# Decayed running sum of a matmul: w loaded by slot over all quadrants, four heads in both first chunks, finer pieces of input

## The chip, the core and the metric

One core of a Trainium2 chip runs the whole kernel. Times are device microseconds (us) of one execution. "The span" is the time from the first to the last instruction in a profiled execution; it is some 2 us shorter than the run's time. In profile lines PE is TensorE and PEld its weight loads, DVE is VectorE, ACT ScalarE, POOL GpSimd and SP SyncE; `a<-b` reads "a is written from b", and [1.25 <-X] says that the engine idled for 1.25 us until X.

## The reference

```python
# x: (16, 2048, 1024), w: (1024, 1024), decay: (1024,), all float32
xw = x @ w
out[:, 0, :] = xw[:, 0, :]
for t in range(1, S):
    out[:, t, :] = decay[None, :] * out[:, t - 1, :] + xw[:, t, :]
```

A matmul is followed by a first-order recurrence along time, with one decay per column. The sixteen batches of 2048 times are cut into 64 chunks of 512 times. Two chunks make a group, and the 1024 output columns are cut into 8 heads of 128. A "step" is one head of one group: 8 slices of w by 2 chunks, 16 matmuls of 512 columns.

## The kernel before

w is cut into 16 slots: slot i is output half h = i // 8, parity e = i // 4 % 2 of its rows, and m = i % 4. x goes through GpSimd's DMA queue (stored as bf16), is turned by VectorE, and is parted into even and odd rows by a copy. w goes through SyncE's queue (the first two slots, kept in f32) and GpSimd's queue (the other fourteen, stored as bf16), into a staging room; a copy by VectorE or ScalarE then "settles" a slot into its place. In the kernel before, each load of w serves ONE quadrant of 32 partitions and several slots at once:

```python
def load_w(queue, h, e, m0=0, m1=M):                  # M = 4
    for q in range(NQ):                               # four transfers, 32 rows each
        pin(queue.dma_start(
            out=stage[h, e, m0][quad(q)].rearrange("p (m d) -> p m d", m=m1 - m0),
            in_=_ap(w, [[2 * D, P], [2 * P * D, m1 - m0], [1, CH]],
                    (q * CQ + m0 * 2 * P + e) * D + h * CH)))
...
for _ in range(34):                                   # warm-up of TensorE
    pin(nc.tensor.matmul(out=spare, lhsT=idle[:, 0:128], rhs=idle, start=True, stop=True))
load_w(nc.sync, 0, 0, 0, M // 2)
...
agenda = {                                            # order of the work off TensorE
    -99: "M0 M1 U0 U1 M2 M3 U2 U3 L L L W0 w1 E0 F0 G0 w3 W2 E1 F1 G1 W4 w5 W6 w7 E2 F2 D G2 E3 F3 G3 W8 W9 W10 W11",
    0: "w12 L L w13 P0 S0",
    ...
```

In the agenda M is a half chunk of x loaded, U a part of w loaded, L a later load of x, E or T a turn, F, G, X, Y a parting, W and w a settle by VectorE and by ScalarE, P, S, C and B the pairing, scan, completion and turning back of one tile. TensorE works on four heads of chunk 0, then on three of chunk 1, as the program gives one of its PSUM tiles of 128x512 to the squared decays; the fourth head's chunk 1 waits for a tile (1.25 us at 27.59 in before's trace).

## Time and profile before

| | before |
|---|---|
| median of 3 runs | 915.26 us (915.03 to 915.39) |
| span of the profiled run | 912.5 us |
| mean granted clock of TensorE | 0.996 |

The prediction shows the page's shares and TensorE's timeline. The DMA view of the first 40 us, in which each digit or number is one microsecond: the busy share of the 16 DMA engines in tenths, and GB/s.

```profile
DMA  0079899999999999999999999999999999999989
GB/s 0 16 241 153 145 226 119 173 180 193 197 197 200 203 181 190 150 191 190 190 195 183 202 201 211 179 187 196 195 196 197 197 195 196 197 196 127 162 97 122
```

From 5 us on the engines are busy for nine tenths or more (once eight), and from 9 to 35 us almost every microsecond moves 180 to 210 GB/s. GpSimd's first eight transfers, issued 0.56 to 0.72 us apart, land 0.66 to 0.93 us apart (6.12 to 11.20).

Then the page's DMA issues (name, queue, count, KB each as stored, and the median us from issue to landing), and two rows of GpSimd's timeline (start, length, line, what it issues, how many, and the wait ahead of it):

```profile
xb<-in_x_dram POOLq DMA_DIRECT2D x16, 128.0 KB, 5.0
ot<-in_w_dram POOLq DMA_DIRECT2D x12, 128.0 KB, 5.2
ot<-in_w_dram SPq DMA_DIRECT2D x4, 128.0 KB, 3.5
```

```profile
6.40 0.76 POOL L245 DMA_DIRECT2D ot<-in_w_dram  x1 [0.39 <-DMA xb<-in_x_dram]
12.01 4.69 POOL L105 DMA_DIRECT2D xb<-in_x_dram  x8
```

GpSimd issues its ninth transfer at 6.40, after the first has landed, and can begin chunk 1's x at 12.01. In the trace its transfers use eight semaphores in turn (99 to 106), and from the ninth on each issue waits for the semaphore of the one eight before it. So eight are in flight by the program's own waits, and the landing of the oldest sets when the next one starts.

And one row of the table by stage for the long middle (stretch, length, busy time and count of PE, PEld, DVE, ACT, POOL, then clock, DMA share and GB/s):

```profile
145.00:880.00 735.00, 731.42 (x3339) 333.20 (x3406) 676.99 (x480) 569.42 (x772) 537.42 (x599) 1.00 1.17 229
```

3406 weight loads in 735 us is a matmul every 0.2158 us, without a break.

### The profile page before, as it was taken

Reading aid. Unit: us, or ns where it says so; the run is one execution under the profiler, and the core shown is the slowest. Engines: PE = TensorE matmul, PEld = TensorE weight load, DVE = VectorE, ACT = ScalarE, POOL = GpSimd, SP = SyncE. Lnnn points to the kernel's source line nnn. Section 1 sums busy time; section 2 is a strip of 40 time slices with the busy share of each in tenths; the row PEclk is TensorE's granted clock in tenths of the full one; section 3 lists DMA queues with packets and bytes.
Section 4 is the critical chain, followed back from the end, with each engine's and each line's share of the span. In section 5 each row is a group of like instructions: output and inputs, shape, how many; then the busy total and the mean of one; then the engine's idle time right before and its main releaser. Section 6 shows DMA issues by size and latency. Waiting matters only on the chain.

```text
span 912.5 us, 11926 instructions
## 1 busy us (share of the span) xinstructions
PE 891.3 (98%) x4088; PEld 408.5 (45%) x4170; DVE 826.0 (91%) x613; ACT 685.8 (75%) x950; POOL 664.4 (73%) x764
## 2 busy tenths in 40 slices
PE   8899999999999999999999999999999999999995
PEld 4444444444444444444444444444444444444442
DVE  4999999999999999999999999999999999999986
ACT  3778887877877777778778778778778778777753
POOL 8688878777777777777677777777787776776552
PEclk9999999999999999999999999999999999999998
DMA  9999999999999999999999999999999999999668
GB/s 170 166 220 215 215 230 235 256 250 255 247 237 255 247 237 224 230 233 231 223 235 227 224 231 229 230 226 231 227 224 230 231 230 224 232 229 207 151 151 219
DMA packets 406253, 204.49 MB, mean 224 GB/s; under 512 B 12976, under 2 KB 405936, under 8 KB 406192
## 3 DMA queue, kind: packets, MB, share of 16 engines
q1 hardware_dynamic: 268848, 134.76, 59.5%
q0 software_dynamic: 137344, 68.96, 56.8%
q8 instruction: 32, 0.52, 0.2%
q14 instruction: 29, 0.24, 0.1%
HBM read 138.42 MB, written 134.22 MB: 299 GB/s over the span
## 4 chain that ended last, share of the span: by engine, by line
PE 90%; DMA 3%; POOL 2%; issue 2%; DVE 2%; ACT 1%; SPq 0%; DVEq 0%; POOLq 0%
PE ps L126 90%; DMA xb<-in_x_dram 2%; POOL xb L105 1%; DMA ot<-in_w_dram 1%; DVE so L194 1%; DVE xw L115 1%; POOL ot L245 1%; PE spare L126 0%; DMA out_dram<-ot 0%; DVE so L180 0%; POOL so L208 0%; ACT xt L123 0%; DVE ot L215 0%; POOL xs L174 0%; ACT xs L168 0%
## 5 line engine op out<-in xcount | busy, mean ns | idle before, releaser
L126 PE MATMUL ps<-xt,wsb 128*128 128x512 bf16 (+1 forms) x4011 | 874.2, 377 | 9.0 <-DVE so L194 2.6
L126 PEld LDWEIGHTS <-wsb 128*128 128x128 bf16 x4136 | 404.6, 98 | 485.7 <-issue 5.6
L174 POOL TENSOR_TENSOR xs<-h,xs 128x512 f32<-128x512 f32 (+1 forms) x193 | 245.3, 1271 | 195.5 <-ACT h L158 88.3
L168 ACT COPY xs<-ps 128x1024 f32<-128x1024 f32 (+1 forms) x193 | 191.6, 993 | 158.8 <-PE ps L126 149.3
L215 DVE STREAM_TRANSPOSE ot<-so 128x1024 f32<-128x1024 f32 (+1 forms) x264 | 302.7, 1184 | 1.9 <-POOL so L208 1.1
L208 POOL TENSOR_TENSOR so<-h,xs 128x512 f32<-128x512 f32 (+1 forms) x193 | 244.3, 1266 | 34.5 <-ACT h L158 18.1
L123 ACT COPY xt<-xw 128x2048 bf16<-128x2048 bf16 (+1 forms) x128 | 239.8, 1875 | 7.5 <-DVE xw L115 7.5
L105 POOL DMA_DIRECT2D xb<-in_x_dram x264 | 174.1, 660 | 2.0 <-POOLq L435 0.9
L158 ACT ACTIVATE h<-so,dec 128x512 f32<-128x512 f32 (+1 forms) x193 | 147.1, 763 | 36.0 <-DVE so L180 32.1
L115 DVE STREAM_TRANSPOSE xw<-xb 128x2048 f32<-128x2048 f32 (+1 forms) x66 | 146.7, 2222 | 6.1 <-DMA xb<-in_x_dram 6.1
L180 DVE TENSOR_TENSOR_SCAN so<-dec,keep,xs 128x512 f32<-128x512 f32 (+1 forms) x99 | 121.6, 1229 | 29.8 <-POOL xs L174 29.6
L180 DVE TENSOR_TENSOR_SCAN so<-dec,xs 128x512 f32<-128x512 f32 x94 | 114.8, 1222 | 31.3 <-POOL xs L174 28.2
L158 ACT ACTIVATE h<-ps,dec 128x512 f32<-128x512 f32 (+1 forms) x193 | 131.8, 683 | 0.0
L194 DVE TENSOR_TENSOR_SCAN so<-dec,ps 128x1024 f32<-128x1024 f32 x33 | 74.5, 2261 | 0.0
L194 DVE TENSOR_TENSOR_SCAN so<-dec,keep,ps 128x1024 f32<-128x1024 f32 (+1 forms) x33 | 73.4, 2225 | 0.0
L211 ACT COPY keep<-so 128x1 f32<-128x1 f32 x136 | 25.1, 187 | 0.3 <-DVE so L194 0.3
L173 ACT COPY so<-keep 128x1 f32<-128x1 f32 x99 | 19.0, 192 | 0.7 <-DVE ot L215 0.7
L171 POOL MEMSET so<- 128x1 f32 x94 | 11.0, 117 | 3.2 <-DVE ot L215 3.2
L262 PE MATMUL spare<-idle 128*128 128x512 bf16 x34 | 10.2, 473 | 1.2 <-DVE idle L259 1.2
L126 PE MATMUL spare<-xt,wsb 128*128 128x512 bf16 (+1 forms) x43 | 11.2, 359 | 0.1
L245 POOL DMA_DIRECT2D ot<-in_w_dram x16 | 9.0, 561 | 2.4 <-issue 0.7
L253 ACT COPY wsb<-ot 128x512 bf16<-128x512 bf16 x6 | 3.4, 615 | 5.7 <-DMA ot<-in_w_dram 5.7
(18 smaller groups left out, 20.3 us busy)
## 6 DMA issues: line engine op xcount, KB each, us to landing
out_dram<-ot SPq DMA_DIRECT2D x248, 512.0 KB, 10.6
xb<-in_x_dram POOLq DMA_DIRECT2D x248, 256.0 KB, 7.8
out_dram<-ot SPq DMA_DIRECT2D x12, 256.0 KB, 4.2
xb<-in_x_dram POOLq DMA_DIRECT2D x16, 128.0 KB, 5.0
ot<-in_w_dram POOLq DMA_DIRECT2D x12, 128.0 KB, 5.2
out_dram<-ot SPq DMA_DIRECT2D x8, 128.0 KB, 2.8
ot<-in_w_dram SPq DMA_DIRECT2D x4, 128.0 KB, 3.5
ot<-in_w_dram POOLq DMA_DIRECT2D x4, 64.0 KB, 4.3
```

What stands on the lines that cost most here:

```text
L105: pin(nc.gpsimd.dma_start(out=xb_of[c][quad(q), j0:j1], in_=_ap(x, [[D, P], [P * D, j1 - j0], [1, CQ]], (b * S + t0 + j0 * P) * D + q * CQ)))
L115: pin(nc.vector.transpose(out=dst.rearrange("p (m j i) -> p j m i", m=M, i=P)[:, j0:j1], in_=src.rearrange("p (j m c) -> p j m c", m=M, c=P)))
L123: pin(copy(out=xt_of[c][:, m0:m1, :, j0 * P:j1 * P], in_=src))
L126: pin(nc.tensor.matmul(out=ps[:, t0:t1], lhsT=wsb[:, k, n].rearrange("p q i -> p (q i)"), rhs=xt[:, k // 2, k % 2, t0:t1], start=(k == 0 a ...
L158: pin(nc.scalar.activation(out=h, in_=src, func=mybir.ActivationFunctionType.Copy, scale=dec[:, self.n:self.n + 1]))
L168: pin(nc.scalar.copy(out=self.xs, in_=self.ps))
L174: pin(nc.gpsimd.tensor_tensor(out=self.xs[:, 1:T:2], in0=g, in1=self.xs[:, 1:T:2], op=ALU.add))
L180: pin(nc.vector.tensor_tensor_scan(out=so[:, 3:T + 2:2], data0=dec2[:, n:n + 1].to_broadcast([128, T // 2]), data1=self.xs[:, 1:T:2], init ...
L194: pin(nc.vector.tensor_tensor_scan(out=so[:, t:t + size], data0=dec[:, n:n + 1].to_broadcast([128, size]), data1=ps, initial=before, op0=A ...
L208: pin(nc.gpsimd.tensor_tensor(out=so[:, 2:T + 2:2], in0=h, in1=self.xs[:, 0:T:2], op=ALU.add))
L211: pin(nc.scalar.copy(out=self.keep, in_=so[:, T + 1:T + 2]))
L215: pin(nc.vector.transpose(out=self.ot[:, :, n % R * P:(n % R + 1) * P], in_=self.so[:, 2:T + 2].rearrange("p (i t) -> p i t", t=P)))
```

## The change

The intent is to start earlier and to lose less in the first 65 us. w comes slot by slot, so that a slice can be settled as soon as its 128 rows are there; the squared decays move out of PSUM until step 7, so all four heads get a PSUM tile for both first chunks; input is turned and parted in halves of the former pieces; the second group is worked on chunk by chunk in its first step (step 8); and the agenda of steps 0 to 16 is made anew.

```diff
-    dec2 = psp.tile([128, 512], FP32, name="dec2")
+    squares = [const.tile([128, K], FP32, name="squares")]
...
-    def turn(c, j0=0, j1=NJ):
+    def turn(c, j0=0, j1=NJ, m0=0, m1=M):
...
-    def load_w(queue, h, e, m0=0, m1=M):
-        for q in range(NQ):
-            pin(queue.dma_start(
-                out=stage[h, e, m0][quad(q)].rearrange("p (m d) -> p m d", m=m1 - m0),
-                in_=_ap(w, [[2 * D, P], [2 * P * D, m1 - m0], [1, CH]],
-                        (q * CQ + m0 * 2 * P + e) * D + h * CH)))
+    def load_w(queue, i):
+        h, e, m = i // 8, i // 4 % 2, i % 4
+        m0 = M // 2 if (h, e) == (0, 0) and m >= M // 2 else 0
+        pin(queue.dma_start(
+            out=stage[h, e, m0][:, (m - m0) * CH:(m - m0 + 1) * CH],
+            in_=_ap(w, [[CQ * D, NQ], [2 * D, P], [1, CH]], (m * 2 * P + e) * D + h * CH)))
...
-    for _ in range(34):
+    pin(nc.scalar.copy(out=idle[:, 0:1], in_=idle[:, 1:2]))
+    for _ in range(27):
...
-    load_w(nc.sync, 0, 0, 0, M // 2)
+    load_w(nc.sync, 0)
+    load_w(nc.sync, 1)
...
-            for j0, j1 in halves:
-                for i in range(3):
-                    for k in range(K):
-                        matmul(heads[i][:, TL:T], i, k, xt_of[1], j0 * P, j1 * P, j0 * P)
+            for k0 in range(0, K, 4):
+                for i in range(R):
+                    for k in range(k0, k0 + 4):
+                        matmul(seconds[i], i, k, xt_of[1], 0, H * P)
+            for i in range(R):
+                for k in range(K):
+                    matmul(seconds[i], i, k, xt_of[1], H * P, TL, H * P)
... (agenda of steps -99 and 0 to 16, order of chunk 0's matmuls, sorting of step 8, stores by outlets: cut)
```

## The prediction

215.8 ns is the distance of two weight loads in the middle of before, and 0.427 us that in its warm-up. What speaks for rival A is the decay loads of before, with one early and four late semaphore updates each (6.05 to 6.29 us for the first), where each load of x shows sixteen; that a slot of w runs on four engines is the assumption. The sum came to 2.3 us gained, so 913.0 us, with all sixteen engines at work.

> **What bounds the kernel now.** I read the page's busy shares and slices first, then the table by stage, then TensorE's and VectorE's timelines of the first 66 us, then the DMA issues. The page first:
>
> ```profile
> span 912.5 us, 11926 instructions
> PE 891.3 (98%) x4088; PEld 408.5 (45%) x4170; DVE 826.0 (91%) x613; ACT 685.8 (75%) x950; POOL 664.4 (73%) x764
> ...
> PE   8899999999999999999999999999999999999995
> ...
> PE 90%; DMA 3%; POOL 2%; issue 2%; DVE 2%; ACT 1%; SPq 0%; DVEq 0%; POOLq 0%
> ```
>
> TensorE is busy everywhere but in the first two slices and the last, and carries 90% of the chain that ended last. So the middle can't be shortened by better overlap. How full the middle is, the table by stage tells (columns: stretch, length, then busy time and count of PE, PEld, DVE, ACT, POOL, clock, DMA share, GB/s):
>
> ```profile
> 73.05:471.00 397.95, 396.05 (x1808) 180.44 (x1844) 370.55 (x264) 311.55 (x421) 300.86 (x339) 1.00 1.22 236
> 471.00:871.63 400.63, 398.63 (x1820) 181.62 (x1857) 367.80 (x261) 312.01 (x422) 291.15 (x325) 1.00 1.14 222
> ```
>
> Some matmul records are missing, so I count weight loads (PEld), one per matmul: 1844 + 1857 = 3701 in 798.58 us, 0.2158 us each, without a break. The program has 64 chunks x 8 heads x 8 slices of w = 4096 full matmuls. The same table gives 100 and 38 loads after 871.63, so 4096 - 3701 - 138 = 257 full matmuls' worth were done before 73.05; at 0.2158 us that is 55.5 us of work. It began at 11.20, so 61.85 us went by: 6.4 us were lost. Those 6.4 us, plus what an earlier start than 11.20 gives, are all this change can win. TensorE's timeline says where:
>
> ```profile
> 1.20 10.17 PE L262 MATMUL spare<-idle 128*128 128x512 bf16 x34 [1.20 <-DVE idle L259]
> 11.20 0.49 PE L126 MATMUL ps<-xt,wsb 128*128 128x256 bf16 x3
> ...
> 14.89 0.49 PE L126 MATMUL ps<-xt,wsb 128*128 128x256 bf16 x3 [0.83 <-DVE xt L123]
> ...
> 20.64 5.70 PE L126 MATMUL ps<-xt,wsb 128*128 128x256 bf16 x48 [0.39 <-DVE xt L123]
> 27.59 1.89 PE L126 MATMUL ps<-xt,wsb 128*128 128x512 bf16 x7 [1.25 <-DVE so L194]
> 29.77 7.07 PE L126 MATMUL ps<-xt,wsb 128*128 128x512 bf16 x32 [0.29 <-DVE so L194]
> 37.69 27.79 PE L126 MATMUL ps<-xt,wsb 128*128 128x512 bf16 x125 [0.86 <-DVE so L194]
> 65.71 0.59 PE L126 MATMUL ps<-xt,wsb 128*128 128x512 bf16 x2 [0.23 <-DVE so L194]
> ```
>
> Up to 20.64 TensorE waits for w and x (0.83, 0.39, and 0.77 at 13.01 for a settled w, a line left out). At 27.59 the fourth head's second chunk has no PSUM tile until head 0's is scanned (1.25), and three more waits for scans follow (0.29 + 0.86 + 0.23): 4.6 us visible, the other 1.8 in switching and pauses too short to be listed. VectorE's timeline shows what it was doing:
>
> ```profile
> 8.60 1.25 DVE L115 STREAM_TRANSPOSE xw<-xb 128x1024 f32<-128x1024 f32 x1 [1.55 <-DMA xb<-in_x_dram]
> 9.88 0.69 DVE L123 COPY xt<-xw 128x1024 bf16<-128x1024 bf16 x1
> ...
> 18.61 1.25 DVE L115 STREAM_TRANSPOSE xw<-xb 128x1024 f32<-128x1024 f32 x1 [2.38 <-DMA xb<-in_x_dram]
> ...
> 25.26 4.45 DVE L194 TENSOR_TENSOR_SCAN so<-dec,ps 128x1024 f32<-128x1024 f32 x2
> ```
>
> It waits for transfers until 19, then has a queue of scans. So the head is bound by transfers first, by VectorE and PSUM after.
>
> [...] 215.8 ns in the middle, and the weight loads of the warm-up stand 0.427 us apart until 6.3 us. [...] The trace agrees for the decay loads, whose slowest dimension is 4: each shows four late semaphore updates where the others show sixteen. The new w transfer reads [4, 32, 512] and writes [128, 512][...]. No run yet shows it for that shape. This is the largest doubt below.
>
> **The change part by part.**
>
> Warm-up: 34 matmuls become 27. Seven fewer at 0.2158 us end it 1.5 us earlier, at 9.7.
>
> First input: a half chunk is turned in two pieces. A transpose of 2048 columns took 2.29 us and one of 1024 1.25, so 1.04 per 1024 and some 0.2 fixed: a piece of 512 should take 0.72 (estimate), and its copy, half of 0.69, some 0.37. From the landing (8.5, by the semaphore of its DMA): 8.6 + 0.72 + 0.37 = 9.7. That is just where the shorter warm-up ends, so whoever cut it expected the landing not to move. Start 11.20 -> 9.7. But the next four matmuls and the second half wait for the second load (11.20 now), so this 1.5 us alone mostly becomes a wait of 1.9 us at 10.6 to 12.5. Finer pieces cost four more transposes, 4 x 0.2 = 0.8 us of VectorE, in time in which it waits for transfers anyway.
>
> w by slot: the bytes are the same, in 14 transfers of 128 KB as stored and two in f32 of 256 KB, in place of 16 and 4. GpSimd has eight in flight: its ninth issue waits for the first landing (6.40 after 6.12), and so on. In the saturated stretch its queue lands 128 KB per 0.67 us. With the second x load at 11.20, six slots follow at 0.67 (15.2; now 15.6), then chunk 1's halves at 17.9 and 20.6 (now 18.5 and 21.2), then the other slots until 26.6. About 0.6 us earlier, if all 16 engines are used.
>
> TensorE in chunk 0 then runs 12.5 -> 18.9 (28 of its 32 matmuls' worth, 6.0 us, and a pause of 0.4 for slot 2); chunk 1's first half starts at 18.1 + 0.72 + 0.37 = 19.2 and its 32 half-width matmuls take 3.5; the second half's input (20.6) is parted by 23.2, just in step, so 3.5 more end at 26.2 with all FOUR heads. Before, that point was 29.5: three heads at 26.3, a wait of 1.25, then 1.9 of matmuls. The freed PSUM bank (the squared decays move to SBUF) is what buys this: 3.3 us.
>
> Step 4 then waits. Its tile is head 0's, scanned from about 24.5 for 2.25 after three settles of w; that is a pause of some 0.3. Its second slice of w is slot 12, which ScalarE settles only after copying head 2 (25.9 to 27.5, then 0.62): TensorE idles some 1.25 to 28.2. Given back: 1.6. From there steps 4 to 7 run unbroken, and step 6 starts at 34.7, where it was 37.69: 3.0 ahead. In step 8 chunk 3's second half is parted about 0.5 after it is wanted; sorting by chunk keeps this to 0.5 (interleaved, its first pair would already wait for chunk 3). A further 0.2 at step 11. The old waits of 0.86 and 0.23 go (the 0.86 is in the 3.0). Sum: 3.0 - 0.5 - 0.2 + 0.2 = 2.5 us ahead at step 14. VectorE has 30 x 1.2 us of work from 25 to 65 with little idle, and starts its scans only some 0.8 earlier than now; I take off 0.2 for waits I can't place. Gain with 16 engines: 2.3 us.
>
> ScalarE's table load (1.28 at 6.59 now) moves ahead of the first w: off the path. Squares in SBUF, then PSUM again: one operation of 0.17. The tail, from the last matmul's end at 901.6 to 912.5, has the same order and the same stores (the list of halved tiles is empty): no change.
>
> **The rivals.**
>
> A: w on 4 engines. Two f32 slots put 128 KB on each of four engines instead of 32 KB on each of sixteen. In the saturated stretch an engine moves 195/16 = 12.2 GB/s as stored, twice that as read, so 96 KB more are up to 3.9 us there; the slack before 11.2 absorbs perhaps half. Six bf16 slots on groups of four engines leave eight engines 16 KB over the mean, 1.3 us more. Chunk 1's halves land 2 to 3 us later than in my sum, and the whole head with them: -2.3 + 2 to 4.5, about 0 to 2 us SLOWER than now. [...] Against: the warm-up fitted to an unmoved first landing, and that the transfers may be split otherwise for 128 partitions. I give it 35%.
>
> B: VectorE becomes the bound. It has about 3.26 us of work for TensorE's 3.45 per step, so it makes up only 0.2 per step; if TensorE runs 3 us ahead, unpaired tiles' scans (steps 7, 11, 15) hold their PSUM tiles and each can give some back. Then only what VectorE starts earlier is won: some 1 us, 914.3. For: the last four waits of before all end with a scan. Against: those scans had been held by steps that are now reordered.
>
> C: settles wait less than I think, w 12 comes in time: the 1.25 doesn't appear, gain 3.5 to 4: 911.5.
>
> **Range and chances.** With 16 engines 915.26 - 2.3 = 913.0; with four, 915.3 to 917.3; C 911.5. I put down 913.0 and 910.8 to 916.8. All that can be won is 6.4 + 1.5 = 7.9 us, under 1%, and to lose 18 us every transfer of the head would have to take twice as long: within 2% is nearly sure, 0.98; 0.01 for each side.
>
> **What would show it.** TensorE's timeline after: first real matmul at 9.7, a wait of near 2 us at 10.6, all four heads of chunk 1 done at 26.2 with no wait for a scan before that, a wait of about 1.25 inside step 4 for ScalarE's settle, and step 6 starting near 34.7. If instead w transfers' waits grow on VectorE and ScalarE before 20 us, or chunk 1's first transpose starts at 20 rather than 18, rival A holds. If waits for scans add over 1 us between 37 and 70, B does. The sum is wrong if the middle isn't 0.2158 us per matmul or the tail isn't 10.9.

## The result, and the profile after

| | before | after |
|---|---|---|
| median | 915.26 us (5 runs, 913.81 to 915.55) | 925.26 us (5 runs, 924.32 to 925.49) |
| ratio, 95% interval | | 1.011 (1.0095 to 1.0125) |
| span of the profiled run | 912.5 us | 923.7 us |
| mean granted clock | 0.996 | 0.988 |

The changed kernel is 10 us slower: within 2%, but far above the range of the prediction.

The middle is the same. Here is the row of the table by stage that answers to the one above:

```profile
145.00:880.00 735.00, 731.45 (x3339) 332.85 (x3406) 678.35 (x479) 572.76 (x773) 539.69 (x603) 1.00 1.17 229
```

Again 3406 weight loads in 735 us. Counted from the first weight load of step 34 to the end, the span is between 777.2 and 778.2 us in before, in after and in all thirteen experiments. So everything that differs lies in the head. The page shows it in its first two slices, which are 23 us each (the share of PE, the clock in tenths, and the packets of the whole run):

```profile
PE   6799999999999999999999999999999999999995
...
PEclk8899999999999999999999999999999999999998
...
DMA packets 411541, 204.51 MB, mean 221 GB/s; under 512 B 18264, under 2 KB 411224, under 8 KB 411480
```

The same bytes are moved in 5288 packets more, and all of these are under 512 bytes: 18264, where the page of before has 12976. The DMA view of the first 40 us and the DMA issues:

```profile
DMA  0024899999963667989699999999999999999999
GB/s 0 0 41 104 136 165 213 200 205 189 137 40 49 64 99 106 112 95 83 89 130 134 187 191 195 193 187 142 84 92 102 140 157 185 158 182 174 169 185 196
```

```profile
xb<-in_x_dram POOLq DMA_DIRECT2D x16, 128.0 KB, 7.2
ot<-in_w_dram POOLq DMA_DIRECT2D x14, 128.0 KB, 7.4
ot<-in_w_dram SPq DMA_DIRECT2D x2, 256.0 KB
```

From 11 to 20 us, where before moved 150 to 203 GB/s, after moves 40 to 112. At 11 and 12 us the DMA engines are busy for only six tenths and three tenths of the time, though bytes are still to be moved: from 12 to 13 us 5.7 packets of 128 bytes or more are under way on the mean, where before has 19.1. The loads of w on SyncE's queue have lost their time to landing in this view; the decay loads, which show four late updates already in before, have none either.

The semaphore updates in the trace tell more. The packed trace has the time of each update of a transfer's semaphore (`prof` prints the last alone); in before each load of w and of x shows sixteen. SyncE's first slot shows one update at 1.85 us and then four (5.32, 5.37, 6.06, 6.24); its second shows one at 2.48 and four at 11.89 to 12.56. The second of the eight loads of x for chunk 0 (issued at 2.02) shows twelve updates by 7.22 and the last four from 10.37 to 11.81: it seems to wait for what carries w. A slot on GpSimd's queue shows sixteen updates, but in groups of four: the first, issued at 8.02, has twelve between 11.11 and 12.69 and the last four between 17.74 and 18.21. Before, the sixteen updates of a slot's transfer on GpSimd's queue lie within 0.4 to 1.4 us, where these take 7.1. The packets point the same way: while SyncE's two slots move (256 packets of 2048 bytes, 2.2 to 12.6 us), at most six of them are under way at once and four or fewer for 95% of the time; in before the same 256 take from 1.8 to 6.1, up to 19 at once. This is what four engines for each slot would look like. The trace doesn't name a packet's engine, so that each late update stands for one engine in use is my reading from here on; the experiments below test the number of updates.

What that does to GpSimd's queue is in its timeline:

```profile
8.02 0.71 POOL L258 DMA_DIRECT2D ot<-in_w_dram  x1 [2.01 <-DMA xb<-in_x_dram]
12.10 0.69 POOL L258 DMA_DIRECT2D ot<-in_w_dram  x1 [3.37 <-DMA xb<-in_x_dram]
16.69 1.40 POOL L105 DMA_DIRECT2D xb<-in_x_dram  x2
```

The ninth transfer is issued at 8.02 in place of 6.40 and the tenth at 12.10, as that second load of x lands only at 11.81. Chunk 1's x can't be issued before 16.69, where it was 12.01, and what the trace gives as landings is this (us):

| | x chunk 0, halves | last slot of w's first half | x chunk 1, halves | last slot of w | x chunk 2 |
|---|---|---|---|---|---|
| before | 8.5, 11.2 | 15.6 | 18.5, 21.2 | 27.1 | 32.4 |
| after | 13.8, 16.0 | 23.5 | 25.8, 28.7 | 39.3 | 43.6 |

VectorE and TensorE follow. VectorE's timeline, and TensorE's:

```profile
13.95 0.71 DVE L115 STREAM_TRANSPOSE xw<-xb 128x512 f32<-128x512 f32 x1 [7.26 <-DMA xb<-in_x_dram]
...
25.92 0.71 DVE L115 STREAM_TRANSPOSE xw<-xb 128x512 f32<-128x512 f32 x1 [2.67 <-DMA xb<-in_x_dram]
...
34.27 2.28 DVE L194 TENSOR_TENSOR_SCAN so<-dec,ps 128x1024 f32<-128x1024 f32 x1
```

```profile
2.28 8.81 PE L275 MATMUL spare<-idle 128*128 128x512 bf16 x27 [2.28 <-ACT idle L273]
15.18 0.80 PE L126 MATMUL ps<-xt,wsb 128*128 128x256 bf16 x3 [4.08 <-DVE xt L123]
...
36.60 0.38 PE L126 MATMUL ps<-xt,wsb 128*128 128x512 bf16 x1 [1.44 <-DVE so L194]
40.28 34.92 PE L126 MATMUL ps<-xt,wsb 128*128 128x512 bf16 x147 [3.31 <-ACT wsb L265]
```

TensorE's first real matmul runs at 15.18, which was 11.20, so 3.98 us later. Counted as in the prediction (full matmuls' worth done, at 0.2158 us each, against the time that went by), before loses 6.4 us after its start and after loses 13.7, 7.3 more. 3.98 + 7.3 is 11.3, against a difference of 11.2 in the spans. The account closes.

Three things make up the second term: waits in chunks 0 and 1; the 1.44 + 3.31 at 36.60 and 40.28, where step 4 waits for head 0's scan and for the settle of slot 12, both late because x and w landed late; and a granted clock of 0.50 in two stretches, 14.8 to 21.7 and 38.7 to 45.6, each beginning near the end of a long pause (of 4.08 and of 3.31 us). The matmuls of 256 columns at 15.18 show it: three take 0.80 us, where before had 0.49.

### The profile page after: what moved, and what is told of

It is laid out like the page before. It is cut to its first block, busy times and chain, and to the rows that moved or that the text cites. A ratio compares the mean times of both kernels' runs of the same rounds, so it can differ in the third digit from the quotient of the medians.

```text
span 923.7 us, 11911 instructions
## 1 busy us (share of the span) xinstructions
PE 895.2 (97%) x4081; PEld 409.0 (44%) x4163; DVE 828.8 (90%) x621; ACT 687.2 (74%) x956; POOL 666.3 (72%) x762
## 2 busy tenths in 40 slices
DMA packets 411541, 204.51 MB, mean 221 GB/s; under 512 B 18264, under 2 KB 411224, under 8 KB 411480
## 4 chain that ended last, share of the span: by engine, by line
PE 93%; DMA 3%; issue 1%; POOL 1%; DVE 1%; ACT 0%; DVEq 0%; POOLq 0%
PE ps L126 93%; DMA ot<-in_w_dram 2%; DMA xb<-in_x_dram 1%; POOL ot L258 1%; PE spare L126 0%; DVE ot L219 0%; DVE so L194 0%; POOL xb L105 0%; ACT wsb L265 0%; POOL xs L173 0%; ACT xs L167 0%; ACT h L157 0%; DVEq L488 0%; DVEq L219 0%; ACT so L172 0%
## 5 line engine op out<-in xcount | busy, mean ns | idle before, releaser
L179 DVE TENSOR_TENSOR_SCAN so<-spare,keep,xs 128x512 f32<-128x512 f32 (+1 forms) x99 | 121.7, 1230 | 30.6 <-POOL xs L173 30.3
L179 DVE TENSOR_TENSOR_SCAN so<-spare,xs 128x512 f32<-128x512 f32 x90 | 110.0, 1222 | 30.7 <-POOL xs L173 27.7
L172 ACT COPY so<-keep 128x1 f32<-128x1 f32 x99 | 18.9, 191 | 2.9 <-DVE ot L219 2.9
L126 PE MATMUL spare<-xt,wsb 128*128 128x512 bf16 (+1 forms) x58 | 14.0, 357 | 0.1
```

What stands on the lines that cost most here:

```text
L126: pin(nc.tensor.matmul(out=ps[:, t0:t1], lhsT=wsb[:, k, n].rearrange("p q i -> p (q i)"), rhs=xt[:, k // 2, k % 2, t0:t1], start=(k == 0 a ...
L179: pin(nc.vector.tensor_tensor_scan(out=so[:, 3:T + 2:2], data0=squares[-1][:, n:n + 1].to_broadcast([128, T // 2]), data1=self.xs[:, 1:T:2 ...
```

## The experiments

Thirteen kernels ran. Three theories stood against each other: that w by slot runs on four engines and that this is the loss; that the loss, or the missing gain, comes from the rest of the change (new order, settles, VectorE); and that the clock lost after the pauses is a cause by itself.

### Which part of the change costs the time

**The changed kernel with w by quadrant on both queues** (label e1_quadrants, 5 rounds):

```diff
-    load_w(nc.sync, 0)
-    load_w(nc.sync, 1)
+    load_wq(nc.sync, 0, 0, 0, M // 2)        # load_wq is load_w of before
...
-        -99: "M0 M1 U2 U3 U4 U5 U6 U7 M2 M3 U8 U9 U10 U11 U12 U13 w1 U14 L U15 W0 L L L E0 ...",
+        -99: "M0 M1 U0 U1 M2 M3 U2 U3 w1 L W0 L L L E0 ...",
```

> The changed kernel with one part undone: w is loaded quadrant by quadrant again[...] on both queues; four heads, finer pieces, settle order and step order stay as changed. Theory A (the by-slot transfers run on 4 of 16 engines and alone cost the time; the rest gains what I predicted): 912 to 914 us, second x load landed near 11.2, chunk 1's last piece near 21, no TensorE pause over 2 us, clock 8/8 throughout. Theory B (the new order of settles and pieces costs a good part by itself): 916 to 921.

Measured: 916.34 us (914.5 to 916.84), 1.0009 of before (0.9996 to 1.0021). Landings are those of before: x at 8.3 and 11.1, chunk 1 at 18.9 and 21.7, the last slot at 27.3. TensorE's first real matmul runs at 9.76. The loss is gone, but the time lies in the second range, 916 to 921, and not in the 912 to 914 hoped for: the rest of the change gained nothing.

**The two halves of it**: only SyncE's two slots by quadrant (e2_sync_quadrants), only GpSimd's fourteen (e3_pool_quadrants), 3 rounds each.

> Only the two f32 slots on SyncE's queue go back to quadrants; the fourteen bf16 ones stay by slot. Theory A: the first x loads land near 8.5 and 11.2 again (now 13.8 and 16.0), but the later slots stay slow: slot 15 lands near 34 (now 39.3), time 918 to 922. If the f32 pair alone were the cause: 912 to 915.

> The reverse: fourteen bf16 slots by quadrant, the two f32 slots stay by slot on SyncE's queue. Theory A: first x loads stay late (13.8 and 16.0), everything after lands at the old pace, last slot near 32; time 916 to 919. If GpSimd's transfers alone were the cause: 912 to 915.

Measured: 919.85 us (1.0052, 1.0038 to 1.0066) and 921.31 us (1.0067, 1.0053 to 1.0081). Against 916.34 of the kernel with both by quadrant, GpSimd's fourteen slots cost 3.5 us and SyncE's two cost 5.0; the sum, 8.5, is near the 8.9 that both together cost (925.26 against 916.34). The first run fell into its range (918 to 922), the second took longer than said (916 to 919). The two slots are only 0.5 of the 2.25 MB of these loads, in the types as stored, and cost at least about as much as the fourteen (the intervals of the two ratios overlap, so the order of 3.5 and 5.0 is not clear of noise). They stand ahead of everything: with them by slot x lands at 13.7, with them by quadrant at 8.3.

**The kernel before with w by slot and nothing else** (e4_before_slots, 3 rounds):

```diff
-    load_w(nc.sync, 0, 0, 0, M // 2)
+    load_ws(nc.sync, 0)                       # load_ws is load_w of the change
+    load_ws(nc.sync, 1)
...
-        -99: "M0 M1 U0 U1 M2 M3 U2 U3 L L L ...",
+        -99: "M0 M1 U2 U3 U4 U5 U6 U7 M2 M3 U8 U9 U10 U11 U12 U13 U14 U15 L L L ...",
```

> The kernel before with this one part of the change alone: w by slot on both queues. Theory A: as slow as the changed kernel or slower, 924 to 928, as it lacks the parts that gain. Theory B: under 921.

Measured: 925.67 us, 1.0119 (1.0103 to 1.0134), 10.7 us over the 914.94 of the kernel before. x of chunk 0 lands at 13.5 and 15.5, of chunk 1 at 25.6 and 28.5. So w by slot alone accounts for the whole loss, on the old schedule as on the new.

### Is it the number of engines?

Four bands of 32 rows could cost for another reason than the four engines that I read from four late updates. In the expectations theory A is that reading. The source of each slot was therefore replaced by others of the same size, rows and order: 128 rows in one run, 8 bands of 16, 2 bands of 64. These load wrong rows of w, so the results are wrong (relative error 1.22).

```diff
-            in_=_ap(w, [[CQ * D, NQ], [2 * D, P], [1, CH]], (m * 2 * P + e) * D + h * CH)))
+            in_=_ap(w, [[2 * D, NQ * P], [1, CH]], ...))            # e5_plain_rows
+            in_=_ap(w, [[96 * D, 8], [2 * D, 16], [1, CH]], ...))   # e12_eight
+            in_=_ap(w, [[256 * D, 2], [2 * D, 64], [1, CH]], ...))  # e13_two
```

> The changed kernel with the source of the w transfers alone altered: each by-slot transfer reads 128 rows two apart, [128, 512], in place of [4, 32, 512]. Same destination, bytes, number and order of transfers; the rows are the wrong ones, so the result is wrong on purpose and correctness will fail. Theory A[...]: sixteen late semaphore updates per w transfer, slot 15 landed near 27, time 911.5 to 914, the sum of my prediction. Theory A' (a transfer over all quadrants is slow for another reason, such as 128 destination partitions or its size): near 925 as the changed kernel.

> The changed kernel, with each slot of w read as 8 x 16 rows, the groups 96 rows apart, in place of 4 x 32 (the wrong rows on purpose, all within w; same bytes, same packets of a row each, same order). [...] the transfers on SyncE's queue should show eight late semaphore updates where the changed kernel shows four, x of chunk 1 should land between that of the changed kernel (28.7 us for its second half) and that of the run with 16 engines (23.0), near 25, and the time lie between 916.5 and 925.3, near 919. If only the cut by quadrants matters (four bands of rows, whatever the engines), or if any transfer that is not on all engines pays alike, it is 924 to 926 with landings as in the changed kernel.

> The changed kernel, with each slot of w read as 2 x 64 rows (wrong rows on purpose)[...]. Two late updates on SyncE's transfers; the second slot of w lands some 10 us later than the 12.6 us in the changed kernel, chunk 1 well after 28.7, and the time is clearly over 925.3: 935 or more. If the changed kernel's loss is not one of engines in use but something that a slot by all quadrants costs once, it stays at 924 to 928.

| source of a slot, rows | late updates on SyncE's slots | packets under 512 B | x chunk 0 lands | x chunk 1 lands | time, us | ratio |
|---|---|---|---|---|---|---|
| 128 | 16 | 12912 | 9.2, 11.9 | 19.9, 23.0 | 916.46 | 1.0019 (1.0006 to 1.0031) |
| 8 x 16 | 8 | 14688 | 11.0, 13.6 | 20.4, 23.1 | 916.2 | 1.0016 (0.9999 to 1.0032) |
| 4 x 32 (the change) | 4 | 18264 | 13.8, 16.0 | 25.8, 28.7 | 925.26 | 1.011 (1.0095 to 1.0125) |
| 2 x 64 | 2 | 25428 | 15.2, 20.2 | 30.9, 35.2 | 933.3 | 1.0203 (1.0188 to 1.0219) |

The lines these rest on, from the three experiments' pages in the order of the table, without the change's own:

```profile
DMA packets 406189, 204.49 MB, mean 224 GB/s; under 512 B 12912, under 2 KB 405872, under 8 KB 406128
```

```profile
DMA packets 407965, 204.49 MB, mean 224 GB/s; under 512 B 14688, under 2 KB 407648, under 8 KB 407904
```

```profile
DMA packets 418705, 204.54 MB, mean 219 GB/s; under 512 B 25428, under 2 KB 418388, under 8 KB 418644
```

And TensorE's first real matmuls with two bands, with the wait for x's parting ahead of them:

```profile
16.59 0.80 PE L126 MATMUL ps<-xt,wsb 128*128 128x256 bf16 x3 [6.46 <-DVE xt L123]
```

The slots show 16, 8, 4 and 2 late updates, for 2, 4 and 8 bands as many as there are bands, and the two runs with the fewest are the slow ones: it isn't the cut by bands, as eight bands (916.2) cost nothing beyond sixteen updates (916.46). The dose isn't even, though. With sixteen I expected 911.5 to 914, as the rest of the change was to gain: the loss went and no gain came. With eight updates I expected near 919, and 924 to 926 if the number didn't matter; it was 916.2, as with sixteen. With eight x of chunk 0 still lands 2 us late, but the queue recovers by chunk 1 (20.4 against 19.9); with four (25.8) and two (30.9) it does not. For two I expected 935 or more, and it was 933.3, with the second slot of w landed at 18.3, 5.7 us later than in the changed kernel and not 10: the direction is right, the size under.

The small packets change with the updates too. Beyond the run with sixteen there are 1776, 5352 and 12516 of them; over the fourteen transfers on GpSimd's queue that is 127, 382 and 894 each, which is 8 x 16, 12 x 32 and 14 x 64 to within 2. By my reading of the updates, the first factor is the number of the sixteen engines left without rows and the second the rows for each engine in use. In the trace they have 4 bytes (9824 of that size on GpSimd's queue in after, 4480 in before). What these packets cost by themselves isn't separated by any run here. They are on GpSimd's queue only (with SyncE's slots alone by slot the page counts 12920), so they have no part in the 5.0 us of SyncE's two slots.

### Where the rest of the change's gain went

With w back by quadrant the change should have won 2.3 us; e1_quadrants won nothing. Its TensorE timeline says where it waits:

```profile
25.06 0.60 PE L126 MATMUL ps<-xt,wsb 128*128 128x256 bf16 x4 [1.11 <-DVE xt L123]
```

VectorE's settle of slot 8 stood ahead of the last two pieces of chunk 1, and waited until 24.38 for its transfer. Three kernels move settles and pieces on top of e1_quadrants, 5 rounds each; a fourth takes work from VectorE.

```diff
 e7_slot8_later, on e1:   -  ... E6 G13 W8 F12 E7 ... D W9 W10 W11
                          +  ... E6 G13 F12 E7 ... D W8 W9 W10 W11
 e8_settles_moved, on e7: -  step 1: "w13 w14 S0",  2: "... S2 w12 B0",  3: "L C0 w15 C1 C2 T2"
                          +  step 1: "S0 W12 w14 W13 w15",  2: "... S2 B0",  3: "L C0 C1 C2 T2"
 e9_chunk3_sooner, on e8: -  step 4: "P4 S3 X2 B2 B1 L T3 Y2",  6: "L P5 L B3 L L T4 P6 X3 Y3 S5 C4"
                          +  step 4: "P4 S3 X2 T3 B2 B1 L Y2",  6: "L P5 X3 L B3 L L T4 Y3 P6 S5 C4"
 e11_relief, on e8:       VectorE turns back only half of each of tiles 8 to 39; the half is
                          stored twice (wrong on purpose, relative error 0.354)
```

> w by quadrant on both queues, as in the first experiment, and VectorE's settle of slot 8 moved from before the last two pieces of chunk 1 to after them: by quadrant, slot 8 lands with its group at 24.3, and held those pieces back. If that hold is what ate the predicted gain: chunk 1 done some 2 us earlier and 913 to 914.5. If VectorE and ScalarE bound the steps after (rival B): the pause moves to step 4 or 8 and the time stays 915 to 916.5.

> As the one before, and the settles of slots 12 to 15 are shared: 12 and 13 on VectorE after head 0's scan, 14 and 15 on ScalarE ahead of head 2's copy, so that step 4 doesn't wait for ScalarE. If step 4's wait was the last of it: 912 to 913.5. If rival B holds: the pause reappears in step 8, where ScalarE parts chunks 2 and 3, and the time is that of the one before.

> As e8, and chunk 3 is turned on VectorE before the first group's two back transposes, its first part copied on ScalarE before head 6's, so that step 8 doesn't wait for it. If only the place of these was at fault: step 8 keeps its lead of 2.7 us over the kernel before, 912.5 to 914. Rival B (VectorE and ScalarE are full there, whatever the order): the waits move to steps 9 to 30 and the time stays 915 to 917.

> As e8, and VectorE turns back only half of tiles 8 to 39 (0.55 us less for each; the half is stored twice, so the transfers' bytes stay; wrong on purpose). Rival B (VectorE is what takes back TensorE's lead after step 9): the waits for scans at steps 11 and 21 to 26 go, step 34 starts 1.6 to 2 us sooner than in e8, time 914 to 915.5. If the lead is lost to something other than VectorE's work: 916 to 917 as e8.

| | time, us | ratio | step 4 | step 8 | step 34 |
|---|---|---|---|---|---|
| before | 915.12 | 1 | 29.10 | 44.38 | 134.56 |
| e1_quadrants | 916.34 | 1.0009 (0.9996 to 1.0021) | 29.09 | 43.86 | 134.97 |
| e7_slot8_later | 915.96 | 1.0013 (1.0 to 1.0025) | 27.47 | 47.52 | 137.30 |
| e8_settles_moved | 916.76 | 1.0025 (1.0011 to 1.0038) | 27.23 | 41.69 | 136.74 |
| e9_chunk3_sooner | 917.07 | 1.0021 (1.0008 to 1.0034) | 26.96 | 41.43 | 137.86 |
| e11_relief | 916.87 | 1.002 (1.0008 to 1.0033) | 28.50 | 42.88 | 138.48 |

(The three last columns are the us of the step's first weight load in the profiled run; the time of before is that of the call of e7 and e8; in e1's call it was 914.94 and in that of e9 and e11 915.14.) None of the four gained: e7 came out where rival B put it, e8 within noise of e7, e9 0.1 us above B's range; a wait taken away in one place came back in another. With e8_settles_moved TensorE enters step 8 at 41.69, 2.7 us ahead of before, and by step 34 it is 2.2 behind. Its timeline:

```profile
45.27 1.02 PE L126 MATMUL ps<-xt,wsb 128*128 128x512 bf16 x4 [1.48 <-ACT xt L123]
47.07 4.48 PE L126 MATMUL ps<-xt,wsb 128*128 128x512 bf16 x20 [0.78 <-ACT xt L123]
52.37 7.10 PE L126 MATMUL ps<-xt,wsb 128*128 128x512 bf16 x31 [0.82 <-DVE so L194]
```

It waits 1.48 and 0.78 for the parting of chunk 3, then 0.82 for a scan. Before has unbroken steps here, at the same work. VectorE starts its first scan at 25.77 (before 25.26), and between that and 140 us it is idle for 4.3 us in all (before 5.1). It starts to turn chunk 3 at 41.02, where before did at 38.70, with no idle time of its own since 37.55. TensorE ran ahead of an engine that had not started earlier and had next to no idle time to catch up in. That speaks for VectorE as what takes the gain back.

e11_relief doesn't test it. VectorE's first halved turning back starts at 68.55; up to there it does the same work as in e8_settles_moved, and the lead is lost before that: steps 8 to 10, 10.36 us without a wait, took 13.91 in e8. In e11 chunk 3 was waited for longer, and the clock fell after it:

```profile
46.93 1.02 PE L126 MATMUL ps<-xt,wsb 128*128 128x512 bf16 x4 [1.94 <-ACT xt L123]
```

A wait of 0.78 followed. From 49.0 to 52.4 the granted clock was 0.50 in that run, and step 9 took 4.8 us in place of 3.45. VectorE's idle time to 140 us rose to 16.4, but step 34 began 1.7 us later than in e8 and not the 1.6 to 2 sooner that B called for.

**A cost that I had overlooked** stands in these traces. In before the squared decays lie in PSUM, and none of the 193 scans that read them takes over 1.29 us, though a GpSimd operation runs beside 121 of them for over 0.6 us. In the changed kernel and what was built on it, the first four such scans read squares from SBUF, and in each run one or two of the four last 1.5 to 3.4 us. The operation that squares again for PSUM takes 1.12 to 1.15, where the first squaring, with no arithmetic on GpSimd beside it, takes 0.17 (at 32.28 in after). In e9_chunk3_sooner (VectorE twice, GpSimd, TensorE), and the scan at the like place in before:

```profile
48.10 3.39 DVE L179 TENSOR_TENSOR_SCAN so<-squares,xs 128x512 f32<-128x512 f32 x1
55.84 1.12 DVE L309 TENSOR_TENSOR spare<-dec 128x8 f32<-128x8 f32 x1
49.12 1.28 POOL L208 TENSOR_TENSOR so<-h,xs 128x512 f32<-128x512 f32 x1
53.72 2.29 PE L126 MATMUL ps<-xt,wsb 128*128 128x512 bf16 x5 [3.26 <-DVE so L194]
```

```profile
49.74 1.19 DVE L180 TENSOR_TENSOR_SCAN so<-dec,xs 128x512 f32<-128x512 f32 x1
```

In all runs but e8 and e11, where one scan of the two differs, the long scan starts while a GpSimd operation runs and ends 1.1 us after it (here at 51.49, GpSimd's at 50.40); the squaring ends within 0.04 us of GpSimd's end in each. It looks as if they wait for GpSimd. Over 1.19 and 0.17 this adds 1.8 us to VectorE's work in e1, 2.3 in e8 and 3.2 in e9, and in e9 the long scan stands just ahead of the scan that TensorE waits 3.26 for. So a full VectorE is the likeliest holder of the gain, and squares in SBUF a part of why it is full; but no run put the squares back into PSUM or relieved VectorE before step 8, so the share of either is not shown.

### Does the clock cost by itself?

Two kernels fill TensorE's pauses in the changed kernel with matmuls of zeros. e6_fill adds warm-ups (46 in place of 27) and 16 idle matmuls at the start of step 4. e10_zeros adds 12 half-width ones before chunk 1's last matmul and 14 after step 4's first two, adding zeros into open sums.

```diff
 e6_fill:   -for _ in range(27):
            +for _ in range(46):
            +    if step == R: 16 x matmul(out=ps[:, 0:TL], lhsT=idle, rhs=idle, start=True, stop=True)
 e10_zeros: +12 x matmul(out=seconds[i][:, H * P:TL], lhsT=idle, rhs=idle[:, 0:H * P], start=False, stop=False)
            +14 x matmul(out=ps[:, 0:TL], lhsT=idle, rhs=idle, start=False, stop=False)
```

> The changed kernel with idle matmuls in two pauses: 46 in place of 27 at the start, and 16 at the start of step 4, so that TensorE has no pause over 2 us before 46 us. Theory C (the half clock after the two long pauses costs time by itself): 922.5 to 923.5, the second cold stretch (13 matmuls at 0.427) gone. If the clock costs nothing beside the waits: 925.

> The changed kernel, and zeros are added into open sums while TensorE would pause: 12 half-width ones ahead of chunk 1's last matmul, 14 after step 4's first two. They wait for nothing new. Theory C (the pause before step 4 halves the clock for 13 matmuls, 2.7 us, which nothing hides): step 5 starts at 43.0 in place of 45.7, time 922 to 923.5. If something else would have bound there: no change, 925.

e6_fill: 923.59 us (4 runs, 923.45 to 927.28), 1.0102. Its profiled run is the slowest of the four; there the 16 matmuls themselves waited 3.47 us for head 0's scan and ran at half clock (the granted clock from 30 to 50 us was 0.83). The other three took 923.45 to 923.68, under each of the changed kernel's five (924.32 to 925.49), and two of them show a mean clock of 0.996 and 0.997, as before does: next to no half clock in the head. They are still over 8 us above the kernel before (915.12). So the clock's share is at most some 2 of the 10 us (an estimate: 925.26 - 923.5).

e10_zeros removed the second stretch of half clock (the granted clock from 30 to 50 us was 1.00, where after has 0.83), and this row shows 73 matmuls from 39.38 on at full speed:

```profile
39.38 16.14 PE L126 MATMUL ps<-xt,wsb 128*128 128x512 bf16 x73
```

Step 5 began at 42.18, 3.5 us before the changed kernel's 45.69; the span ended 1.7 us sooner and the timed runs not at all (925.53 us, 1.0114, 1.0099 to 1.013), which is the second of its two expectations. New waits of 0.37, 0.36 and 0.35 in the steps to 68 us are part of what it gave back. Here, then, the half clock came with the pauses (with the second one filled, 1.00 in place of 0.83), and it is not what makes up the most of the 10 us: e12_eight too had a clock of 0.84 from 15 to 30 us, at 916.2.

No version that ran beats the kernel before. The best with right results, e1_quadrants and e7_slot8_later, are the same as it.

## Why the prediction was wrong, point by point

- **Middle and tail.** Right: 0.2158 us per matmul in both, and an unchanged end.
- **w on sixteen engines, the number put down.** Wrong, and this is the step that failed. The rival (A), at 35%, fits what happened: four late updates on SyncE's slots, and 16, 8 and 2 with other sources of the same size (916.46, 916.2 and 933.3 us). Undoing it brings 925.26 back to 916.34.
- **The size of rival A.** Also wrong, and this is why the range missed. It was sized by the bytes on the most loaded engine, with "the slack before 11.2 absorbs perhaps half": chunk 1 2 to 3 us later, 0 to 2 us slower in all. Measured, chunk 1 landed 7.3 and 7.5 us later than before, the last slot 12.2, and the time grew by 10. The term left out is the queue: the program has eight of GpSimd's transfers in flight, the issue eight later waits for a transfer's last update, and so a load of x whose last four updates came late (10.37 to 11.81) held the tenth issue until 12.10, while the DMA engines stood idle for more and more of the time (at 12 us the busy share is three tenths). There was no slack: x of chunk 0 itself landed 5.3 us late. The small packets (5288 more than before) weren't foreseen either.
- **"The warm-up fitted to an unmoved first landing."** Unsound as an argument against A. The warm-up waits for ScalarE's copy into the idle tile and starts at 2.28, not 1.20, so its 27 matmuls end at 11.1 in after, not at 9.7. I had counted the matmuls and not looked at what the first one waits for. That the first real matmul ran at 9.76 in e1_quadrants is luck: its warm-up takes 7.64 us, as the full clock was granted from 5.64 on. In e5, e7 and e8, with the same warm-up and the clock from 6.6 to 6.7 on, it ran at 10.54, 10.24 and 10.29.
- **The cost of pieces.** Right: 0.71 for a transpose (0.72 said), 0.43 for VectorE's copy (0.37).
- **All four heads by 26.2, with sixteen engines.** With w by quadrant off by one to three: step 4 began at 29.09 in e1_quadrants and at 27.23 with the settles moved. Chunk 1 landed at 18.9 and 21.7, not the 17.9 and 20.6 of my sum: w by quadrant or by plain rows, the queue landed nothing over 0.3 us sooner than before. (The 26.6 for the last slot was short by its own rates too: the part of chunk 2's x ahead of it has 256 KB and lands in 1.35 us, not 0.67.)
- **A pause for ScalarE's settle in step 4.** Right in kind: it is there in after (3.31, as w was late) and in e7_slot8_later (2.87). I said 1.25. In e1_quadrants it was 0.45.
- **Step 6 at 34.7.** Reached by e8_settles_moved (34.78) and e9_chunk3_sooner (34.53), by their first weight load. But the lead wasn't kept, and here **rival B** was nearer than my sum: "VectorE starts its scans only some 0.8 earlier" was false in every run that I read it from (25.51 at best, against 25.26 before). I named the cap and then didn't apply it; and the 3.26 us of VectorE's work per step is by the lines shown 3.2 (370.55 of 397.95 us busy). The 2.3 us were a sum over TensorE's waits alone. What remains open is whether VectorE alone is that cap, as e11_relief came too late to test it.
- **"Squares in SBUF, then PSUM again: one operation of 0.17."** Wrong: that operation took 1.13 to 1.15, and one or two scans of the squares in SBUF 1.5 to 3.4 in place of 1.2. What this is worth in the run's time is not shown.
- **The clock.** Not foreseen at all. It fell to 0.50 by the end of the long pauses (4.08 and 3.31 us), yet taking the second stretch away gained nothing in the timed runs, and with next to none left (e6_fill's two runs) 8 of the 10 us stayed. The share of the first stretch alone stays open.

## What to carry to other kernels

Before cutting a transfer differently, look at its shape and at the semaphore updates of transfers already in the trace: a slot of 128 partitions read as 4 x 32 rows showed four late updates here and ran to 925.26 us, read as 128 rows sixteen and 916.46, and the decay loads showed four late ones in the trace of before, ahead of any run. Size such a loss by the queue and not by bytes: what is issued behind the slow transfer, how many may be in flight, and what stands first (two transfers out of sixteen cost 5.0 us here, the other fourteen 3.5). And a gain counted from one engine's waits is worth only what the next busiest engine can start earlier. Where an operand is moved from PSUM to SBUF, look in the first trace at how long its readers take.

## What the traces show of transfers, and of pauses and the clock

- The two queues show a slot of 4 x 32 rows differently in after: on SyncE's, the first has one update early (1.85 us) and four late (5.32 to 6.24); on GpSimd's, the first has sixteen, the last four late (17.74 to 18.21). And on GpSimd's queue such a transfer goes with 382 small packets more than one of 128 rows, one of 8 x 16 with 127, one of 2 x 64 with 894.
- In after the ninth of GpSimd's transfers was issued at 8.02, after the first landing at 7.73, and the tenth at 12.10 after 11.81, with eight in flight by the program's semaphores. The time was 1.1% longer than before; with eight late updates on SyncE's slots (916.2) nothing could be told from sixteen (916.46).
- Pauses of TensorE and the clock: with the pause of 4.08 us in after, the granted clock was 0.50 from 14.8 to 21.7. Shorter pauses went with half clock as well: 3.31 in after (38.7 to 45.6), 1.94 and 0.78 with four matmuls between them in e11_relief (49.0 to 52.4), and a single one of 1.71 with plain rows (13.5 to 16.9); 1.63 in e1_quadrants did not. So in this case the length of a pause alone doesn't tell, and what decides is not shown.
